# Log-sum-exp over rows: an earlier range check, and two bulk loads as four transfers each to move the store to another semaphore

## The chip, the cores and the metric

One core of a Trainium2 chip. The metric is the device time of one execution in microseconds (us); several are taken (the first six of the kernel before lie between 164.22 and 164.74 us). The profiled span is about 1.8 us shorter than the time of the same run (163.0 us for 164.74 before). By the record every timed run that is compared below was in the fast state with a granted clock of 1.0; the three runs taken once each are listed there as "unknown".

## The reference, cut to what matters

```python
x = randn(32, 512, 1024)           # float32, 67.1 MB
max_x = max(x, axis=-1, keepdims=True)
out = max_x + log(sum(exp(x - max_x), axis=-1))     # float32 (32, 512)
```

## The kernel before

The 16,384 rows lie as 128 partitions x 128 columns, one row of 1,024 numbers to each. Columns are loaded in 17 loads of 16 down to 1 columns into a ring of 48. ScalarE (ACT) takes exponentials in place, VectorE (DVE) sums them ("R": one reduction over several rows; "T": a row's two halves added with an accumulator), and some rows ACT sums itself ("A"). In the profile PE is TensorE and PEld its weight loads, POOL is GpSimd, and a q behind an engine's name (SPq, DVEq) stands for its sequencer, under whose name the profile lists waits, jumps, register loads and the issuing of transfers (EVENT_SEMAPHORE, COMPARE_BRANCH, TENSOR_LOAD, DMA_DIRECT2D). There is no subtraction of the maximum on this fast path. Instead a range check at the end decides whether the sums can be trusted; if not, a branch runs the exact form.

```python
loads = ["R8 R8", "R8 R8", "R8 R8", "R7 R6 A A", ..., "R3 A", "R2 T2", "R3", "R1 A", "T2", "T1", "A", "A"]

def load(p0, c0, size):
    return nc.sync.dma_start(out=ring[:, p0 : p0 + size, :], in_=x_rows[:, c0 : c0 + size, :])
# ... cut: for each load the exponentials and sums; at finalize the first load is moved
#     ahead of the opening barrier (start_early)
nc.scalar.activation(out=res[:, EARLY:NC], in_=sumexp[:, EARLY:NC], func=AF.Ln)   # last 24 columns
nc.sync.dma_start(out=out_view, in_=res)                                          # the store

nc.vector.tensor_scalar(out=clamped[:, 0:LAST], in0=sumexp[:, 0:LAST],            # LAST = 127
    scalar1=LOW, scalar2=HIGH, op0=ALU.max, op1=ALU.min)
nc.vector.scalar_tensor_tensor(out=clamped[:, 0:LAST], in0=clamped[:, 0:LAST], scalar=0.0,
    in1=sumexp[:, 0:LAST], op0=ALU.bypass, op1=ALU.not_equal, accum_out=bad[:, 0:1])
nc.tensor.matmul(count, lhsT=bad[:, 0:1], rhs=far, start=True, stop=False)
# ... cut: a test of the last row, its product, and the product of the last column's sum
nc.vector.tensor_scalar(out=fine, in0=count, scalar1=HIGH, scalar2=None, op0=ALU.is_lt)
all_fine = nc.values_load(fine[0:1, 0:1], engines=ENGINES, ...)   # register load on ACT and DVE
with tc.If(all_fine < 1, ...):       # the exact form; not taken with this data
```

The transfers signal eight semaphores in turn (102, 103 and 105 to 110 in the records; numbered 0 to 7 here), with 16 completion events for each transfer; the last of the 16 is what I call its landing. At the end of the program SyncE (SP), which issues all 18 transfers, waits for the eight, in the order (number 2; then 1 and 3; 0 and 4; 5; 6; 7; from 160.68 to 162.09 us in the kernel before), and then for the closing barrier. By the trace's records three of these waits also hold a semaphore of the check: 5 and 6 come with those of the flag's two register loads, 7 with one of DVE's. Before, the store is the 18th transfer and signals semaphore 1; what comes after it in SP's list is four more waits.

## Time and profile before

| what | value | where it is read |
|---|---|---|
| time, median of 6 runs | 164.48 us (164.22 to 164.74) | the runs |
| profiled span | 163.0 us | the page |
| load queue, share of 16 engines | 96.4% | the page, DMA queues |
| DVE / ACT busy | 75% / 72% | the page |
| last load landed | 158.82 us | the trace's completion events |
| from there to the end of the span (below: the tail) | 4.14 us | the same |

The page of the kernel before, first its busy line, then packets and queue:

```profile
PE 0.4 (0%) x6; PEld 0.2 (0%) x6; DVE 122.0 (75%) x44; ACT 116.7 (72%) x53; POOL 0.2 (0%) x4
...
DMA packets 2594, 67.19 MB, mean 412 GB/s; under 512 B 288, under 2 KB 416, under 8 KB 800
...
q1 hardware_dynamic: 2592, 67.18, 96.4%
```

The load queue has work nearly the whole time (96.4%, against 75% for the busiest engine): the kernel is bound by its loads. The 288 packets under 512 B are as many as the completion events, 16 for each of 18 transfers; I call them the semaphore packets. In the trace's packet records such a packet (4 bytes) takes 9 ns in the median, and a row run of 65,536 bytes takes 2.418 us on its engine.

Next the timeline of the end of the kernel before. The columns are start in us, length in us, engine, line, operation, what it writes and reads, how often, and in brackets the idle time before and what ended it:

```profile
158.50 0.69 DVE L106 SCALAR_TENSOR_TENSOR ring<-ring 128x512 f32<-128x512 f32 x1
...
158.87 1.01 ACT L92 ACTIVATE last_exp<-ring 128x1024 f32<-128x1024 f32 x1
159.12 0.09 DVE L106 DVE_READ_ACCUMULATOR ring<-ring 128x1 f32 x1
159.31 0.23 DVE L142 TENSOR_SCALAR clamped<-sumexp 128x127 f32<-128x127 f32 x1
159.57 0.29 DVE L146 SCALAR_TENSOR_TENSOR clamped<-clamped,sumexp 128x127 f32<-128x127 f32 x1
159.79 0.08 DVE L146 DVE_READ_ACCUMULATOR clamped<-clamped,sumexp 128x1 f32 x1
159.79 0.21 DVE L151 TENSOR_REDUCE bad<-ring 128x1 f32<-128x64 f32 x1
...
160.03 0.22 ACT L136 ACTIVATE res<-sumexp 128x24 f32<-128x24 f32 x1
...
160.28 0.35 SPq L137 DMA_DIRECT2D out_dram<-res  x1
...
160.52 0.14 DVE L158 TENSOR_SCALAR fine<-count 1x1 int32<-1x1 f32 x1 [0.33 <-PE count L156]
```

Two branches leave this picture. The store branch is the last exponential, the logarithm and the store. The check branch is the last DVE add, the check, the flag, then a register load and a jump. The timeline stops at the flag (160.66 us), although the span goes on to 162.96: register loads, jumps and semaphore waits do not count as busy, and the page's chain of waits ends there too. They have to be asked for by line. This is the register load of the flag in the kernel before (duration in ns, then start):

```profile
L159 ACTq TENSOR_LOAD <-fine x1: 506/506/506, 160.7 to 160.7; - x1
L159 DVEq TENSOR_LOAD <-fine x1: 657/657/657, 160.7 to 160.7; - x1
```

And this, from the waits of SP in the kernel before (us in total, times, longest), is what it waits for in the closing line:

```profile
SPq L223 <- DMA out_dram<-res: 1.1, 1, 1.1
```

The store landed at 161.82 us. The records of SP's remaining waits and its drains stand about 62 ns apart, so that SP reaches the closing barrier at 162.19, and DVE, after its jump, at 162.26. The barrier is collected by POOL from 162.29 on and costs 0.67 us. **The end of the span is set by the later of the two branches, and they are 64 ns apart.**

### The profile page before, as it was taken

What the parts mean: (1) busy time and instruction counts of PE and PEld (TensorE: products, weight loads), DVE (VectorE), ACT (ScalarE), POOL (GpSimd) and SP (SyncE); (2) the same over time, 40 slices, a digit from 0 to 9 for tenths busy, and PEclk for the clock granted to TensorE, in tenths of its full rate; (3) what the DMA queues carried; (4) which work ended last, traced back from release to release, by engine and by line L of the source; (5) the groups of instructions that cost most, each with busy time, mean ns of one, the idle gap of its engine ahead of it and who ended that gap; (6) DMA issues with size and microseconds to landing.
All of it is one profiled execution on the core that took longest, in us unless ns stands there. A gap on an engine that the chain in (4) does not pass through costs nothing.

```text
span 163.0 us, 198 instructions
## 1 busy us (share of the span) xinstructions
PE 0.4 (0%) x6; PEld 0.2 (0%) x6; DVE 122.0 (75%) x44; ACT 116.7 (72%) x53; POOL 0.2 (0%) x4
## 2 busy tenths in 40 slices
PE   0000000000000000000000000000000000000001
PEld 0000000000000000000000000000000000000000
DVE  0000000899959999499999995999997999979893
ACT  3000059980899509993599749999969599999993
POOL 0000000000000000000000000000000000000000
DMA  8997998899899899989999979999999999999970
GB/s 306 467 515 338 434 515 386 386 515 418 354 515 418 354 499 483 392 362 452 450 450 450 450 322 483 382 417 407 434 434 458 402 428 420 430 417 421 412 294 20
DMA packets 2594, 67.19 MB, mean 412 GB/s; under 512 B 288, under 2 KB 416, under 8 KB 800
## 3 DMA queue, kind: packets, MB, share of 16 engines
q1 hardware_dynamic: 2592, 67.18, 96.4%
q14 instruction: 2, 0.02, 0.0%
HBM read 67.11 MB, written 0.07 MB: 412 GB/s over the span
## 4 chain that ended last, share of the span: by engine, by line
DMA 64%; DVE 22%; ACT 12%; issue 0%; PE 0%; DVEq 0%
DMA ring<-in_x_dram 64%; DVE sumexp L101 20%; ACT ring L94 12%; DVE ring L106 1%; DVE clamped L142 0%; PE count L155 0%; DVE bad L152 0%; DVE clamped L146 0%; DVE fine L158 0%; DVE bad L151 0%; PE count L156 0%; DVEq L142 0%
## 5 line engine op out<-in xcount | busy, mean ns | idle before, releaser
L101 DVE TENSOR_REDUCE sumexp<-ring 128x8 f32<-128x8192 f32 (+7 forms) x20 | 116.2, 5854 | 37.3 <-ACT ring L94 37.3
L94 ACT ACTIVATE ring<-ring 128x8192 f32<-128x8192 f32 (+7 forms) x24 | 101.7, 4282 | 42.7 <-DMA ring<-in_x_dram 42.7
L92 ACT ACTIVATE ring<-ring 128x1024 f32<-128x1024 f32 x12 | 12.5, 1039 | 0.0
L106 DVE SCALAR_TENSOR_TENSOR ring<-ring 128x512 f32<-128x512 f32 x8 | 5.1, 685 | 0.0
L92 ACT ACTIVATION_READ_ACCUMULATOR ring<-ring 128x1 f32 x12 | 2.2, 186 | 0.0
L67 ACT ACT_TABLE_LOAD x1 | 1.3, 1283 | 0.8 <-PEq L212 0.8
L92 ACT ACTIVATE last_exp<-ring 128x1024 f32<-128x1024 f32 x1 | 1.0, 1007 | 0.0
L68 DVE MEMSET ones<- 128x1 f32 x1 | 0.1, 59 | 0.9 <-PEq L212 0.9
L106 DVE DVE_READ_ACCUMULATOR ring<-ring 128x1 f32 x8 | 0.7, 83 | 0.0
L150 PE MATMUL count<-far,bad 128*1 128x1 f32 x2 | 0.2, 164 | 159.9 <-DVE clamped L146 159.9
L158 DVE TENSOR_SCALAR fine<-count 1x1 int32<-1x1 f32 x1 | 0.1, 145 | 0.3 <-PE count L156 0.3
L146 DVE SCALAR_TENSOR_TENSOR clamped<-clamped,sumexp 128x127 f32<-128x127 f32 x1 | 0.3, 291 | 0.0
L142 DVE TENSOR_SCALAR clamped<-sumexp 128x127 f32<-128x127 f32 x1 | 0.2, 227 | 0.1
L150 PEld LDWEIGHTS count<-far,bad 128*1 128x1 f32 x2 | 0.1, 80 | 159.9 <-DVE clamped L146 159.9
L121 ACT ACTIVATE res<-sumexp 128x104 f32<-128x104 f32 x1 | 0.3, 273 | 0.0
L136 ACT ACTIVATE res<-sumexp 128x24 f32<-128x24 f32 x1 | 0.2, 222 | 0.0
L151 DVE TENSOR_REDUCE bad<-ring 128x1 f32<-128x64 f32 x1 | 0.2, 215 | 0.0
L156 PE MATMUL count<-ones,sumexp 128*1 128x1 f32 x2 | 0.2, 164 | 0.0
L155 PE MATMUL count<-far,bad 128*1 128x1 f32 x2 | 0.2, 164 | 0.1
L92 ACT ACTIVATION_READ_ACCUMULATOR last_exp<-ring 128x1 f32 x1 | 0.2, 185 | 0.0
L152 DVE TENSOR_SCALAR bad<-bad 128x1 f32<-128x1 f32 x1 | 0.2, 154 | 0.0
L156 PEld LDWEIGHTS count<-ones,sumexp 128*1 128x1 f32 x2 | 0.1, 82 | 0.0
(7 smaller groups left out, 0.6 us busy)
## 6 DMA issues: line engine op xcount, KB each, us to landing
ring<-in_x_dram SPq DMA_DIRECT2D x1, 7680.0 KB, 32.8
ring<-in_x_dram SPq DMA_DIRECT2D x1, 7168.0 KB, 30.4
ring<-in_x_dram SPq DMA_DIRECT2D x1, 5120.0 KB, 31.7
ring<-in_x_dram SPq DMA_DIRECT2D x1, 4608.0 KB, 34.3
ring<-in_x_dram SPq DMA_DIRECT2D x1, 4096.0 KB, 29.8
ring<-in_x_dram SPq DMA_DIRECT2D x2, 2048.0 KB, 33.2
ring<-in_x_dram SPq DMA_DIRECT2D x1, 3072.0 KB, 36.7
ring<-in_x_dram SPq DMA_DIRECT2D x2, 1024.0 KB, 39.2
```

The lines of the kernel that those rows point to most:

```text
L67: nc.scalar.preload_act_table_set("natural_log_exp_and_others")
L92: exp = nc.scalar.activation(out=o, in_=v, func=AF.Exp, accum_out=sums)
L94: exp = nc.scalar.activation(out=v, in_=v, func=AF.Exp)
L101: added = [nc.vector.reduce_sum(out=sums, in_=v, axis=AX.X)]
L106: nc.vector.scalar_tensor_tensor(out=lo, in0=lo, scalar=1.0, in1=ring[:, p + r, H:d], op0=ALU.mult, op1=ALU.add, accum_out=sums[:, r : r + 1],
L121: nc.scalar.activation(out=res[:, 0:EARLY], in_=sumexp[:, 0:EARLY], func=AF.Ln)
L136: nc.scalar.activation(out=res[:, EARLY:NC], in_=sumexp[:, EARLY:NC], func=AF.Ln)
L142: nc.vector.tensor_scalar(out=clamped[:, 0:LAST], in0=sumexp[:, 0:LAST], scalar1=LOW, scalar2=HIGH, op0=ALU.max, op1=ALU.min,)
L146: nc.vector.scalar_tensor_tensor(out=clamped[:, 0:LAST], in0=clamped[:, 0:LAST], scalar=0.0, in1=sumexp[:, 0:LAST], op0=ALU.bypass, op1=AL ...
L150: nc.tensor.matmul(count, lhsT=bad[:, 0:1], rhs=far, start=True, stop=False)
L151: nc.vector.reduce_max(out=bad[:, 2:3], in_=last_row[:, 0, 0 : d // 16], axis=AX.X)
L156: nc.tensor.matmul(count, lhsT=sumexp[:, LAST:NC], rhs=ones, start=False, stop=True)
```

## The change

Three things are named: the first load ahead of the opening barrier (the kernel before has this already; the diff only rewrites the test that finds the spot); a range check of 118 of the 127 sums ahead of the last rows, so that only 9 are left for the end; and two bulk loads (columns 32 to 47 and 48 to 62) as four transfers each, which makes six transfers more and thereby brings the store to semaphore 7, the last in SP's list.

```diff
     def load(p0, c0, size):
-        return nc.sync.dma_start(out=ring[:, p0 : p0 + size, :], in_=x_rows[:, c0 : c0 + size, :])
+        step = 4 if c0 in (32, 48) else 1
+        return [
+            nc.sync.dma_start(
+                out=ring[k::step, p0 : p0 + size, :], in_=x_rows[k::step, c0 : c0 + size, :]
+            ).ins
+            for k in range(step)
+        ]
+    def check(c0, c1, i):        # the clamp, the compare and the product, for columns c0 to c1
+        ...
+        if c == LATE + 3:        # LATE = 118
+            check(0, LATE, 0)
...
-        k = next(k for k, i in enumerate(top) if i.engine == SP and "Drain" in type(i).__name__)
+        k = next(k for k, i in enumerate(top) if i.engine == SP and isinstance(i, mybir.InstDrain))
...
-    (clamp, compare and product of columns 0:127)
+    check(LATE, LAST, 1)
```

(The rest of the diff gives `bad` a fourth column and handles a list of transfers in place of one. The call with `LATE + 3` stands behind the last three-row reduction in the text; in the trace below, the check runs ahead of that reduction.)

More of the change, by code (lines that the diff above doesn't have):

```diff
@@ L49 @@
     EARLY = 104
+    LATE = 118
     LAST = NC - 1
@@ L59 @@
     clamped = stats.tile([P, NC], fp32, name="clamped")
-    bad = stats.tile([P, 3], fp32, name="bad")
+    bad = stats.tile([P, 4], fp32, name="bad")
     fine = stats.tile([1, 1], i32, name="fine")
@@ L71, in load @@
     def load(p0, c0, size):
-        return nc.sync.dma_start(out=ring[:, p0 : p0 + size, :], in_=x_rows[:, c0 : c0 + size, :])
+        step = 4 if c0 in (32, 48) else 1
[5 more added lines that the diff above has]
+        ]
     def without_wait(ins, group, reason):
         tc.declare_no_dep(ins.ins, group=group, reason=reason)
+    def check(c0, c1, i):
+        nc.vector.tensor_scalar(
+            out=clamped[:, c0:c1], in0=sumexp[:, c0:c1],
+            scalar1=LOW, scalar2=HIGH, op0=ALU.max, op1=ALU.min,
+        )
+        nc.vector.scalar_tensor_tensor(
+            out=clamped[:, c0:c1], in0=clamped[:, c0:c1], scalar=0.0, in1=sumexp[:, c0:c1],
+            op0=ALU.bypass, op1=ALU.not_equal, accum_out=bad[:, i : i + 1],
+        )
+        nc.tensor.matmul(count, lhsT=bad[:, i : i + 1], rhs=far, start=i == 0, stop=False)
     c = 0
@@ L83 @@
             p = 0
-        dma = load(p, c, size).ins
+        dmas = load(p, c, size)
         if c == 0:
-            first_load = dma
+            first_load = dmas[0]
         for how, s in ops:
@@ L111 @@
             for add in added:
-                tc.declare_no_dep(add.ins, dma, reason="ScalarE has waited for it")
+                for dma in dmas:
+                    tc.declare_no_dep(add.ins, dma, reason="ScalarE has waited for it")
                 without_wait(add, "loads", "they came before this one")
@@ L118 @@
             last_row = v
-        tc.add_to_no_dep_group("loads", dma)
+        for dma in dmas:
+            tc.add_to_no_dep_group("loads", dma)
         if c == EARLY + 14:
             nc.scalar.activation(out=res[:, 0:EARLY], in_=sumexp[:, 0:EARLY], func=AF.Ln)
+        if c == LATE + 3:
+            check(0, LATE, 0)
     def start_early(program):
@@ L130, in start_early @@
         top = blocks[0].instructions
-        k = next(k for k, i in enumerate(top) if i.engine == mybir.EngineType.SP and "Drain" in type(i).__name__)
+        k = next(
+            k for k, i in enumerate(top)
+            if i.engine == mybir.EngineType.SP and isinstance(i, mybir.InstDrain)
+        )
         top.insert(k, first)
@@ L137 @@
     nc.sync.dma_start(out=out_view, in_=res)
+    check(LATE, LAST, 1)
+    nc.vector.reduce_max(out=bad[:, 3:4], in_=last_row[:, 0, 0 : d // 16], axis=AX.X)
     nc.vector.tensor_scalar(
-        out=clamped[:, 0:LAST], in0=sumexp[:, 0:LAST],
-        scalar1=LOW, scalar2=HIGH, op0=ALU.max, op1=ALU.min,
-    )
-    nc.vector.scalar_tensor_tensor(
-        out=clamped[:, 0:LAST], in0=clamped[:, 0:LAST], scalar=0.0, in1=sumexp[:, 0:LAST],
-        op0=ALU.bypass, op1=ALU.not_equal, accum_out=bad[:, 0:1],
-    )
-    nc.tensor.matmul(count, lhsT=bad[:, 0:1], rhs=far, start=True, stop=False)
-    nc.vector.reduce_max(out=bad[:, 2:3], in_=last_row[:, 0, 0 : d // 16], axis=AX.X)
-    nc.vector.tensor_scalar(
-        out=bad[:, 1:2], in0=bad[:, 2:3], scalar1=LOG_LOW, scalar2=None, op0=ALU.is_lt
-    )
-    nc.tensor.matmul(count, lhsT=bad[:, 1:2], rhs=far, start=False, stop=False)
+        out=bad[:, 2:3], in0=bad[:, 3:4], scalar1=LOG_LOW, scalar2=None, op0=ALU.is_lt
+    )
+    nc.tensor.matmul(count, lhsT=bad[:, 2:3], rhs=far, start=False, stop=False)
     nc.tensor.matmul(count, lhsT=sumexp[:, LAST:NC], rhs=ones, start=False, stop=True)
```

## The prediction

> **What bounds it now.** The loads. In the profile page the load queue is busy 96.4% of 16 engines' span (163.0 us) against DVE 75%, ACT 72%. In the trace's DMA records a row run is one packet: 65,536 bytes take 2.418 us, a semaphore packet (4 bytes) 9 ns; 8.4 MB loads land 19.3 us apart (434 GB/s). The last load lands at 158.82 us; ACT starts the last exponential at 158.87. So nothing in the middle can gain; only the ends can.
>
> **The tail now** (timeline and semaphore events, us from the start). Two branches meet at the closing barrier:
> - Store: last exponential 158.87, logarithm 160.03, store issued 160.28, landed 161.82. SP then still goes through four more waits and two drains, about 62 ns each; it arrives at 162.19.
> - Check: last DVE add ends 159.20, range check 159.31 to 159.87, then the last row's test, three products, a flag, a 0.66 us register load and a branch; DVE arrives at 162.26.
> The barrier starts 0.03 us later and costs 0.67 us.
>
> **The change, costed.**
> 1. First load ahead of the barrier: before has it already (its first load issues at 0.00, before SP's drain); the new text selects the same spot. Zero.
> 2. Check of 118 sums: it now stands before the three-row reduction that starts at 152.89. DVE idles 0.77 us there, waiting for ACT; the 127-wide pair took 0.56 us, so it fits and delays nothing. At the end the pair covers 9 columns instead of 127: about 0.06 us off the clamp (227 ns against 154 for one column) and 0.12 us off the compare (about 1.04 ns a column), an estimate of 0.18 us off the check branch. One extra product runs early on an idle PE.
> 3. Eight transfers for two. The store moves from the semaphore that SP awaits second to the one it awaits last; what each load waits for shifts by six semaphores but stays the same load. Gain on the store branch: four waits, about 0.22 us. Cost: 6 semaphore packets an engine, 6 x 9 ns = 0.05 us on the DMA stream and all after it; six SP issues of 0.33 us are hidden, as loads are issued some 30 us ahead of landing.
>
> [...]
>
> **Sum.** Check branch: -0.18 + 0.05 = -0.13; store branch: -0.22 + 0.05 = -0.17. The later one counts: about -0.13 us. Predicted 164.4 us (163.9 to 164.9). Faster by over 2%: 1%; within 2%: 92%; slower: 7%.
>
> **What would show it.** Packets of 65,536 bytes still 2.42 us; 384 semaphore packets; landings from the third load on 0.05 us later; the 118-wide pair inside DVE's idle time near 152 us, reduction start unchanged; SP one wait after the store's landing; DVE's arrival still the later one.
>
> **What would make it wrong.** [...] packets up to twice as long, 10 to 38 us slower (8.4 and 7.9 MB at down to half rate). Or the check delaying the reduction, costing what it saves.

No term of the sum is cut: -0.18 + 0.05 on the check branch and -0.22 + 0.05 on the store branch, of which the later one leaves -0.13 us. Step 3 rested on my assumption that the split loads keep the rate of whole ones (434 GB/s), and "up to twice as long" was an assumption too; the 38 us are an estimate from it, since in the kernel before the two loads landed 19.5 and 18.4 us after the ones ahead of them. The "1.04 ns a column" can be read from the compare's own times: 1.02 ns between 512 and 127 columns before (685 and 291 ns), 1.04 between 118 and 9 after (282 and 169 ns).

## The result, and the profile after

| | before | after |
|---|---|---|
| time, median of 6 runs | 164.48 us | 164.08 us (163.99 to 164.47) |
| ratio of fast runs | | 0.9982, 95% interval 0.9967 to 0.9997 |
| profiled span | 163.0 us | 162.2 us |
| last load landed | 158.82 us | 158.35 us |
| tail | 4.14 us | 3.85 us |

A ratio is the mean time of one kernel's fast runs over that of the other's fast runs of the same rounds, so it is not quite the ratio of the medians quoted.

The page of the changed kernel, the same lines:

```profile
PE 0.6 (0%) x8; PEld 0.3 (0%) x8; DVE 122.3 (75%) x47; ACT 116.8 (72%) x53; POOL 0.2 (0%) x4
...
DMA packets 2690, 67.19 MB, mean 414 GB/s; under 512 B 384, under 2 KB 512, under 8 KB 896
...
q1 hardware_dynamic: 2688, 67.18, 96.8%
```

There are 96 more packets, all under 512 B: the 6 x 16 semaphore packets (the trace has 96 more completion events too, 384). The early check in the timeline of the changed kernel (columns as above):

```profile
151.56 0.08 DVE L127 DVE_READ_ACCUMULATOR ring<-ring 128x1 f32 x1
151.68 0.22 DVE L89 TENSOR_SCALAR clamped<-sumexp 128x118 f32<-128x118 f32 x1
151.94 0.28 DVE L93 SCALAR_TENSOR_TENSOR clamped<-clamped,sumexp 128x118 f32<-128x118 f32 x1
152.14 0.08 DVE L93 DVE_READ_ACCUMULATOR clamped<-clamped,sumexp 128x1 f32 x1
...
152.41 3.35 DVE L122 TENSOR_REDUCE sumexp<-ring 128x3 f32<-128x3072 f32 x1 [0.18 <-ACT ring L115]
```

The pair ends before the three-row reduction could start: DVE still waits 0.18 us for ACT. The end of the changed kernel:

```profile
158.38 1.01 ACT L113 ACTIVATE last_exp<-ring 128x1024 f32<-128x1024 f32 x1
158.64 0.08 DVE L127 DVE_READ_ACCUMULATOR ring<-ring 128x1 f32 x1
158.83 0.17 DVE L89 TENSOR_SCALAR clamped<-sumexp 128x9 f32<-128x9 f32 x1
159.03 0.17 DVE L93 SCALAR_TENSOR_TENSOR clamped<-clamped,sumexp 128x9 f32<-128x9 f32 x1
159.13 0.08 DVE L93 DVE_READ_ACCUMULATOR clamped<-clamped,sumexp 128x1 f32 x1
159.14 0.22 DVE L170 TENSOR_REDUCE bad<-ring 128x1 f32<-128x64 f32 x1
...
159.55 0.22 ACT L164 ACTIVATE res<-sumexp 128x24 f32<-128x24 f32 x1
...
159.80 0.35 SPq L165 DMA_DIRECT2D out_dram<-res  x1
159.88 0.15 DVE L176 TENSOR_SCALAR fine<-count 1x1 int32<-1x1 f32 x1 [0.33 <-PE count L175]
```

From the start of the clamp to the start of the last-row test it is 0.31 us instead of 0.48. The register load of the changed kernel, and what SP waits for in its closing line:

```profile
L177 ACTq TENSOR_LOAD <-fine x1: 467/467/467, 160.1 to 160.1; - x1
L177 DVEq TENSOR_LOAD <-fine x1: 540/540/540, 160.1 to 160.1; - x1
```

```profile
SPq L241 <- DVEq L181: 0.5, 1, 0.5
SPq L241 <- ACTq L181: 0.3, 1, 0.3
SPq L241 <- DMA out_dram<-res: 0.2, 1, 0.2
```

SP now goes through its list while the store is under way, waits 0.2 us for the store at its end, and reaches the barrier 0.146 us after the landing instead of 0.370. DVE's register load is 0.12 us shorter, which I had not predicted. The last load landed 0.48 us earlier, which I had not predicted either. Both needed runs.

### The profile page after: what moved, and what is told of

It reads as the page before. It is cut to its first block, busy times and chain, and to the rows that moved or that the text cites. A ratio compares the mean times of both kernels' runs of the same rounds, so it can differ in the third digit from the quotient of the medians.

```text
span 162.2 us, 216 instructions
## 1 busy us (share of the span) xinstructions
PE 0.6 (0%) x8; PEld 0.3 (0%) x8; DVE 122.3 (75%) x47; ACT 116.8 (72%) x53; POOL 0.2 (0%) x4
## 3 DMA queue, kind: packets, MB, share of 16 engines
q1 hardware_dynamic: 2688, 67.18, 96.8%
## 4 chain that ended last, share of the span: by engine, by line
DMA 64%; DVE 22%; ACT 12%; issue 0%; PE 0%; DVEq 0%
DMA ring<-in_x_dram 64%; DVE sumexp L122 21%; ACT ring L115 12%; DVE ring L127 1%; PE count L174 0%; DVE clamped L89 0%; DVE bad L171 0%; DVE bad L170 0%; DVE clamped L93 0%; DVE fine L176 0%; PE count L175 0%; DVEq L89 0%
## 5 line engine op out<-in xcount | busy, mean ns | idle before, releaser
L93 DVE SCALAR_TENSOR_TENSOR clamped<-clamped,sumexp 128x118 f32<-128x118 f32 (+1 forms) x2 | 0.5, 226 | 0.1
```

What stands on the lines that cost most here:

```text
L93: nc.vector.scalar_tensor_tensor(out=clamped[:, c0:c1], in0=clamped[:, c0:c1], scalar=0.0, in1=sumexp[:, c0:c1], op0=ALU.bypass, op1=ALU.n ...
```

## The experiments

The theory (two branches): the closing barrier waits for the later of store branch and check branch, so each half of the change alone is worth almost nothing, and both together 0.28 us. The theory was formed on the first pair of profiles, so the 0.28 is no forecast; the forecasts are those of the runs below. The first rival (stream): the gain comes from the load stream, which the four-way transfers make steadier, as the earlier landing in the first pair of profiles suggests. The second rival (sum): the halves' gains simply add.

All times in this table count from the landing of the last load, in us, worked out from the trace's records. "SP" and "DVE" are their arrivals at the closing barrier; "register load" is DVE's.

| run | last load landed | SP | DVE | register load | tail | ratio (95%) |
|---|---|---|---|---|---|---|
| before | 158.82 | 3.37 | 3.44 | 0.657 | 4.138 | |
| before again | 158.27 | 3.36 | 3.43 | 0.675 | 4.133 | 1.0002 (0.9987 to 1.0017) |
| check's half | 158.71 | 3.36 | 3.15 | 0.547 | 4.057 | 1.0007 (0.9991 to 1.0022) |
| store's half | 158.53 | 3.15 | 3.42 | 0.670 | 4.120 | 1.0011 (0.9997 to 1.0025) |
| changed | 158.35 | 3.14 | 3.15 | 0.540 | 3.854 | 0.9982 (0.9967 to 0.9997) |
| changed again | 158.34 | 3.16 | 3.14 | 0.546 | 3.851 | 0.9994 (0.9981 to 1.0008) |
| changed, third | 158.57 | 3.14 | 3.13 | 0.537 | 3.838 | 0.9996 (0.9984 to 1.0008) |
| six small loads | 158.71 | 3.17 | 3.14 | 0.534 | 3.867 | 0.9984 (0.9971 to 0.9997) |

### Only the check in two parts

```diff
-        step = 4 if c0 in (32, 48) else 1
+        step = 1
```

> The change's check in two parts, but every load one transfer, so the store sits on the semaphore awaited second, as before. Two-branch theory (the closing barrier waits for the later of store branch and check branch): DVE arrives some 0.25 us earlier, but the store branch (370 ns from landing to SP's arrival) then binds; tail from last load's landing to the end about 4.07 us against 4.14 before and 3.85 with the whole change; time 0.05 to 0.08 us under before (ratio 0.9996). Stream theory (the four-way transfers make the load stream steadier): tail as above, and no gain in time from this half. Sum theory (the two halves' gains add): tail 4.14 - 0.28 = 3.86.

Measured: DVE arrives 0.29 us earlier than before, SP as before, and the tail is 4.057 us. The closing line of this run, from SP's waits, is that of the kernel before:

```profile
SPq L241 <- DMA out_dram<-res: 1.1, 1, 1.1
```

0.29 us off one branch took 0.08 us off the tail. The sum theory, which wanted 3.86, is out.

### Only the store on another semaphore

```diff
-        if c == LATE + 3:
-            check(0, LATE, 0)
...
-    check(LATE, LAST, 1)
+    check(0, LAST, 0)
```

> The loads of the change (two of them as four transfers), the check whole at the end as before. Two-branch theory: SP arrives 0.15 us after the store's landing instead of 0.37, but DVE's arrival binds: tail from last landing to the end still 4.1 us (at most 0.12 us less if the flag's register load takes 0.54 us and not 0.66); six more semaphore packets of 9 ns on the stream; ratio 1.000. Stream theory: last load lands about 0.5 us earlier than in before (158.3 against 158.8 us), packets' excess over their median summed per engine near 1.0 us against 1.35 us; ratio 0.997. Sum theory: tail 3.92.

Measured: SP arrives 0.22 us earlier, DVE at 3.42 us as before, and the tail is 4.120 us. In the closing line SP's longest wait is now the one for DVE's jump:

```profile
SPq L239 <- DVEq L179: 0.7, 1, 0.7
```

The view lists no wait for the store, but by the records it still came last in SP's list: SP arrives 0.146 us after the landing, as in the changed kernel. The two branches are thus not quite separate, since SP's list also holds the register loads of the check; in the changed kernel its wait for ACT's ended 0.22 us before the store landed.

The time did not fall (ratio 1.0011, 0.9997 to 1.0025), so the runs show no gain from the four-way transfers by themselves. The halves are worth 0.08 and 0.02 us of tail alone and 0.28 together.

### The kernel before, once more

```diff
 (no edit)
```

> The kernel before, unchanged, once more. Two-branch theory with a stream that varies from run to run: ratio 1.000; tail from last landing to the end 4.14 us again within 0.03; but the last load's landing varies by some tenths of a microsecond, so that it need not be 158.8 us. Stream theory: landing at 158.8 us and the same excess of packets in the middle of the run (0.7 us per engine after the first 4 us) again, because they come from the whole-load transfers.

Measured: the tail is 4.133 us, within 5 ns, but the last load landed at 158.27 us, 0.55 us earlier than in the first profile of the very same kernel and earlier than in all the profiles of the changed one. The stream theory, which wanted 158.8 us again, is out. (The landings with four-way transfers in the table, 158.34 to 158.57 us, lie within those without, 158.27 to 158.82; eight profiles can't exclude a difference of a tenth or two.) The packet records say where the variation sits: the time of the load packets above their usual length, per engine, was 1.3 us in the first profile and 0.8 in this one, and of that 0.76 against 0.15 us after the first 4 us. It lies in stretches that differ from run to run, in runs with and without four-way transfers. Why they come, no run here shows.

### The changed kernel, once more, and a third time

```diff
 (no edit)
```

> The changed kernel, unchanged, once more. Two-branch theory: ratio 0.998 again, tail 3.85 us within 0.03, DVE and SP arriving within 0.05 us of each other; landing of the last load anywhere within the range that the kernel before shows. Stream theory: landing near 158.3 us again, 0.3 us or more ahead of both profiles of before.

> The changed kernel, a third time, beside the six-small-loads version on one chip, to narrow its ratio. Two-branch theory: tail 3.85 us, and with 0.05 us on the stream a ratio of 0.9985 on average over all its runs (0.23 us of 164.5). If the splitting cost more on the stream than its semaphore packets: ratio nearer 1.000 with the tail unchanged.

Measured: tails of 3.851 and 3.838 us, DVE and SP within 22 ns of each other, now with SP the later. The ratios were 0.9994 and 0.9996, whose intervals reach past 1; the 0.998 and 0.9985 expected lie at their lower ends, the first just outside. A gain of 0.2 us lies at the edge of what five rounds resolve, since the stream alone moves single runs by half a microsecond. Over all 17 runs of the changed kernel the mean is 164.24 us; over all 38 of the one before, its repeat included, it is 164.45, both pooled over chips and rounds. The difference is 0.21 us, give or take 0.12 (1.96 standard errors). The tails (-0.285) and the counted semaphore packets (+0.054) give -0.23.

### The four transfers as blocks of neighbouring partitions

```diff
-                out=ring[k::step, ...], in_=x_rows[k::step, ...]
+                out=ring[k * P // step : (k + 1) * P // step, ...], in_=x_rows[k * P // step : (k + 1) * P // step, ...]
```

> The changed kernel, but each of the four transfers takes 32 neighbouring partitions instead of every fourth: still 16 semaphore packets a transfer. [...] packets of 65,536 and 61,440 bytes in these two loads take up to twice 2.42 and 2.27 us, loads of 8.4 and 7.9 MB land some 37 us apart instead of 19, time about 200 us (180 to 205). Engine-count theory (only the number of engines used matters): packets and time as in the changed kernel, 164.2 us.

The first forecast's factor of two was my assumption, applied to the measured 2.42 and 2.27 us of the packets.

Measured: 205.78 us (one run, just above the 180 to 205 expected), a packet of 61,440 bytes 4.79 us in the median instead of 2.27, and each quarter of the first split load landing some 10.1 us after the one before instead of 4.84. The throughput of 40 slices of this run, from its DMA view:

```profile
GB/s 411 411 411 411 411 411 411 437 270 206 206 206 206 206 206 200 277 217 193 193 193 193 193 337 382 439 410 442 458 398 426 435 430 429 406 427 430 409 408 32
DMA packets 2690, 67.19 MB, mean 329 GB/s; under 512 B 384, under 2 KB 512, under 8 KB 896
```

Half the rate in just the two split loads (206 and 193 GB/s in their slices, against 411 in those ahead of them), with the same 384 semaphore packets and the 16 engines busy for 97.4% of the span by the DMA view (96.8% in the changed kernel): the engine-count theory is out. Why the blocks are slower is not shown: the edit changed both which partitions each transfer writes and which rows of DRAM it reads, and no run separates the two. What is shown is that the step of 4 makes the splitting harmless (quarters of 2.1 MB 4.84 us apart, 433 GB/s); with blocks the kernel is a quarter slower. The tail here is 3.868 us, so the end of the kernel was not touched.

### The first load behind the opening barrier

```diff
-    nc.at_finalize(start_early)
```

> The changed kernel with its first load left behind the opening barrier. If the early load is worth what the trace shows (first load issued at 0.00 us, the second at 0.8 us behind the barrier), everything shifts by 0.7 to 0.8 us: ratio to before 1.003 (about 0.5 per cent over the changed kernel), tail from last landing to the end unchanged at 3.85 us. If the early load is hidden by something else: no difference to the changed kernel, ratio 0.999.

Measured: ratio 1.0028 (1.0002 to 1.0054), tail 3.856 us. The first load is issued 0.73 us after the start of the span. The early start is real, but both kernels had it.

### The flag later

```diff
+    nc.vector.tensor_scalar(out=bad[:, 2:3], in0=bad[:, 2:3], scalar1=1.0, scalar2=None, op0=ALU.mult)
     nc.tensor.matmul(count, lhsT=bad[:, 2:3], rhs=far, start=False, stop=False)
```

> The changed kernel with one idle one-column step more in the check (a multiplication by 1), which makes the flag about 0.25 us later; result unchanged. Overlap theory (the flag's register load on DVE is longer when it ends while the store's packets move, 0.84 to 1.20 us after the store's issue): it starts some 0.5 us after the store's issue and takes 0.66 us instead of 0.54; DVE arrives 0.37 us later, the tail is 3.85 + 0.35 = 4.20 us. Rival (the register load was shorter for some other reason that goes with the early check): it stays 0.54 us, the tail is 4.08 us.

### The store later

```diff
     nc.scalar.activation(out=res[:, EARLY:NC], in_=sumexp[:, EARLY:NC], func=AF.Ln)
+    nc.scalar.activation(out=res[:, EARLY:NC], in_=sumexp[:, EARLY:NC], func=AF.Ln)
```

(on top of the store's half alone)

> The run with the store's half alone (check whole at the end), with the last logarithm done twice, so that the store is issued about 0.25 us later while the check stays as it is; result unchanged. Overlap theory: the flag's register load now starts about 0.15 us after the store's issue, ends before its packets move, and takes 0.54 us instead of 0.67, so DVE arrives 0.12 us earlier (3.30 us after the last landing) although nothing in its branch changed; SP arrives at 3.40 and binds: tail 4.10 us. Rival: the register load stays at 0.67 us and DVE at 3.42; tail 4.12 us.

These two settle the register load. First the flag later in the changed kernel, then the store's half alone, then the same with the store later:

```profile
L180 DVEq TENSOR_LOAD <-fine x1: 640/640/640, 160.5 to 160.5; - x1
```

```profile
L175 DVEq TENSOR_LOAD <-fine x1: 670/670/670, 160.4 to 160.4; - x1
```

```profile
L176 DVEq TENSOR_LOAD <-fine x1: 541/541/541, 160.4 to 160.4; - x1
```

The store's packets move from about 0.85 to 1.2 us after its issue in every run. In all runs DVE's register load takes 0.53 to 0.55 us when it ends before that (at 0.70 to 0.81 us after the issue), and 0.64 to 0.68 us when it ends among them (at 1.06 to 1.09). Nothing in the check branch differs between the last two runs, and moving only the store (by a second logarithm on ACT) took 0.13 us off the register load: DVE arrived at 3.30 us instead of 3.42. SP then bound, at 3.40, with a tail of 4.089 us; 4.10 was expected. With the flag later, the tail was 4.126 us, less than the 4.20 expected: the extra step made the register load start 0.17 us later, not 0.25, and the load itself took 0.10 more. ACT's register load took 462 to 467 ns in the changed kernel and six other runs, in which it ended before or just as the packets began, and 506 ns (the kernel before) and 530 (the flag later) where it ended well among them. That the load is longer when it lasts into the time of the store's packets is shown, by moving either; that the packets themselves hold it up, and by which path, is not.

### Six small loads in place of the splitting

```diff
-        step = 4 if c0 in (32, 48) else 1
+        step = 1
...
+    for i in range(6):
+        nc.sync.dma_start(out=spare[:, 16 * i : 16 * i + 16], in_=x_flat[0:1, 16 * i : 16 * i + 16])
```

> The check in two parts as in the change, all loads whole as before, and six loads of 64 bytes into a spare tile behind the last load, so that the store again comes to the semaphore awaited last. Semaphore theory (only the store's place among the waits matters, not the splitting): tail 3.85 us as in the changed kernel, SP 0.15 us after the store's landing; the six small loads queue behind the loads, so that the stream has none of the 6 x 9 ns: on average 0.05 us better than the changed kernel, ratio 0.998, too little for the time to tell. Split theory (the four-way transfers themselves give something): tail 4.06 us as in the run with the check's half alone, ratio 1.000.

Measured: tail 3.867 us, SP 0.146 us after the landing, ratio 0.9984 (0.9971 to 0.9997). Six transfers of 64 bytes that nobody reads, queued behind the last load, do for the store's semaphore what the splitting does. So the place in SP's list is what matters. Against the changed kernel of the same rounds it is at least as good (median 164.13 against 164.20 us, ranges overlapping); that it is better by the 0.05 us of the semaphore packets is argued, not shown.

## Why the prediction was right

The prediction of 164.4 us (163.9 to 164.9) held; the size of the gain was underestimated by one term. The number alone proves little: the range also holds the 164.48 us of the kernel before, and the 0.40 us between the first medians exceeds the 0.28 us of the tails, as the variation of the stream came on top by luck. The mechanism is tested by the tails.

- **The bound.** Loads bind (96.4 and 96.8% of the queue), and only the ends can gain: the tails account for the whole gain, to the accuracy of the runs (-0.23 us with the semaphore packets, beside -0.21 give or take 0.12).
- **Step 1, first load early: zero.** Right. In both kernels the first load is issued at 0.00 us. Taking the early start out of the changed kernel costs about 0.7 us (it was then 0.51 us slower than the kernel before of its rounds, which the changed kernel beats by 0.21), so it would have been seen had it been new.
- **Step 2, the early check fits into DVE's idle time.** Right: the reduction after it still waits for ACT (0.18 us). The 9-wide pair saved 0.16 us by its two terms (0.057 at the clamp, 0.107 at the compare); 0.18 was estimated.
- **What step 2 missed.** "-0.18" for the check branch measured -0.28: the flag, coming earlier, also brought its register load to an end before the store's packets moved, and the load took 0.12 us less. I had carried the 0.66 us over as a constant. This is the term that was mis-sized.
- **Step 3, the store's semaphore: 0.22 us off the store branch.** Right: 0.370 to 0.146 us from landing to arrival, about 56 ns for each of the four waits.
- **Step 3's condition, that loads split by every fourth partition keep the rate of whole ones.** Right: quarters of 2.1 MB landed 4.84 us apart (433 GB/s, against 434 for whole loads). My reasons for it are not shown. The block run shows that a loss like the one named in "what would make it wrong" was possible with another split: 41 us, a little over the 10 to 38 given for it.
- **Step 3's cost of 0.05 us on the stream.** The packets were counted (384 of 9 ns), but landings "0.05 us later" could not be seen: the stream varies by 0.5 us between runs of one kernel. The first profile even showed landings 0.48 us earlier, which the repeat of the kernel before took back.
- **"DVE's arrival still the later one."** True in the first profile by 18 ns, not in the two repeats (SP by 22 and 10 ns): the extra 0.12 us had brought the branches level. That they came out level is luck, not part of the prediction.
- **The sum.** -0.13 us predicted, -0.21 give or take 0.12 measured over all runs; the times alone can't tell -0.13 from -0.23, the tails can.

## What to carry to other kernels

Where a program ends in a barrier, draw every branch that leads to it, including the waits, register loads and jumps that no busy time counts; here shortening one branch paid only down to the next one, so that two changes worth 0.08 and 0.02 us of tail alone were worth 0.28 together. When a gain is smaller than the variation of the bound itself, measure it as an interval inside the trace that repeats (here the tail, within some 15 ns) and run the unchanged kernel again before believing a shift anywhere else. If a transfer is split over partitions, test a stride before blocks: here every fourth partition kept 433 GB/s and blocks of 32 brought it down to about 206, for a reason that no run shows.
